# A hybrid encoder block on one core: the input projection by seven block products in place of eight, half of the tokens at a time

## The chip, the core and the metric

The kernel runs on one core of a Trainium2 chip. TensorE (PE in the profile) does matmuls and transposes. VectorE (DVE), ScalarE (ACT) and GpSimd (POOL) do the elementwise work. SyncE (SP) starts most transfers; 16 DMA engines carry them between the device memory (DRAM) and the on-chip buffer SBUF. Matmuls accumulate in PSUM, of which one "bank" here is a tile of 128 partitions by 512 float32.

The metric is device time in microseconds of one execution, lower is better. Before the change the median is 2041.7 us over 3 runs (2040.75 to 2042.08).

## The reference

x is 2048 tokens by 1024 channels, w_in has 7168 columns.

```python
h = rms_norm(x, pre_norm_w)
proj = h @ w_in
hy_in, hy_gate, sg_u, sg_v, sg_gate = split(proj, [3*1024, 4*1024, 5*1024, 6*1024])
x0, x1, v = split(short_conv_centred(hy_in, conv_w, conv_b), 3)   # 3 taps along the tokens
k = hyena_filter(...)              # a sine MLP of the position times a decay, both directions
y_a = x0 * long_conv_bidir(v * x1, k, hyena_skip) * silu(hy_gate)  # by Fourier transform
vn = layer_norm(sg_v per head of 128) * w + b
mixed = einsum(sgu_w, vn) + sgu_b  # 128 x 128 mixing of positions in chunks of 128 tokens
y_b = sg_u * mixed * silu(sg_gate)
y = concatenate([y_a, y_b]) @ w_out
out = x + rms_norm(y, post_norm_w)
```

## The kernel before

**Products.** Every wide product is made at more than single-pass precision: `split` (line 147) makes a rounded high part on ACT (line 150) and the remainder on DVE or POOL (line 152), and `mm3` (lines 155 to 159) runs three matmuls, high by high, low by high, high by low. One matmul is 128 x 128 stationary by 128 x 512 moving.

**Projection.** w_in is cut into 56 blocks of 128 output channels. `prep_w` loads a block (512 KB) and splits it, the remainder on POOL. The normalised, transposed x stays in SBUF in four token quarters, `xh[n]` and `xl[n]`. `project(blk, nxt)` takes a block over the quarters in turn: 8 slices of the 1024 input channels, three matmuls each, 24 into one bank, then the consumer reads the bank. That is 96 matmuls a block and 5376 in all.

**Stages.** `x_phase` normalises 16 tiles of 128 tokens on DVE (line 288), transposes them on PE (line 293) and splits them; two blocks run between (`ug_first`). `mlp` makes the hidden layers of the filter. `ug_phase` projects sg_gate and sg_u with `k1_jobs` beside it: 32 jobs, each two filter products (line 454), decay (line 456), sum and difference, l1 norm (line 463, DVE), first Fourier step, result to the DRAM array AK. `xv_phase` projects x1 and v, convolves (line 501), and a first Fourier step sends the product to AU. `xg_phase` does x0 and hy_gate, result to XG. `vb_phase` projects sg_v, normalises (lines 644 to 652), mixes (line 660), and multiplies by the stored sg_u product (line 619). In its background and behind half of `xv_phase`, from `late_jobs`, are 64 `fft_job`s (second Fourier step of AU and of AK, pointwise product on lines 691 and 695, inverse step, to BY) and 32 `inv_job`s (last step, transposed on line 733, times XG, to Y). `first_out` and `out_phase` multiply Y by w_out (1536 matmuls), normalise and add x.

**What sets the order.** The jobs are generators; at each yield of the projection `run` calls `tick`, which moves every active job on by one step and starts `rate` new ones. From there the order of the instructions on each engine is fixed in the program: each engine takes its own row strictly in order, and waits at a semaphore where an operand isn't there. DMAs that SP starts go in one order too.

## Time and profile before

| of the profiled execution | value |
|---|---|
| its own time | 2044.02 us |
| span, first to last instruction | 2042.2 us |
| median of the runs that were timed | 2041.7 us |
| PE busy | 1991.0 us, 97% |
| DVE busy | 1160.2 us, 57% |
| ACT busy | 764.4 us, 37% |
| POOL busy | 230.0 us, 11% |
| moved by DMA | 274.22 MB, mean 134 GB/s |
| granted TensorE clock, mean | 0.995 |

The profiled execution takes 1.8 us more than its span, and 2.3 us more than the median. "Busy" counts an engine as busy from an instruction's start to its end; matmuls overlap, so a matmul of 0.39 us can start 0.23 us behind the last. In rows of a timeline stand the start, the length, the engine, the line, the operation, output<-inputs by the program's names, the shape and a count, and in brackets how long the engine was idle before and what ended it.

### The profile page before, as it was taken

To read this page: it belongs to the slowest core of one execution; us is meant where nothing else is said; L and a number is where in the kernel's file an instruction comes from. 1 tells how busy PE (TensorE), PEld (TensorE's weight loads), DVE (VectorE), ACT (ScalarE), POOL (GpSimd) and SP (SyncE) were. 2 spreads that over 40 slices of the span, in tenths; PEclk is the share of its full clock that TensorE was granted. 3 is DMA by queue.
4 is the path that set the end of the run, shared out by engine and by line. 5 is a ranking of instruction groups with operands and counts; after the bars stand their busy time and mean duration, and the time that the engine had idled before them with its cause. 6 is when DMAs were issued, how large, how long until landed. Compare 5 with 4: busy or idle time off the path is not lost. (4 is left out here: it accounts for less than half of the span.)

```text
span 2042.2 us, 24620 instructions
## 1 busy us (share of the span) xinstructions
PE 1991.0 (97%) x9000; PEld 1618.6 (79%) x9000; DVE 1160.2 (57%) x1906; ACT 764.4 (37%) x1333; POOL 230.0 (11%) x227
## 2 busy tenths in 40 slices
PE   6999999999999999999999999999999999999998
PEld 5777888878888877777777778788788887888887
DVE  7357555663333587778877766665666664323221
ACT  7134434443333455555444444433222343211111
POOL 1011111111000010111111101110000000101000
PEclk9999999999999999999999999999999999999999
DMA  6155535441222455546554455443546555523311
GB/s 214 49 147 179 164 119 171 157 131 47 61 61 62 127 157 153 154 125 191 154 155 140 144 160 166 152 145 117 160 144 200 159 171 172 171 83 97 110 62 42
DMA packets 189705, 274.22 MB, mean 134 GB/s; under 512 B 18027, under 2 KB 93803, under 8 KB 189551
## 3 DMA queue, kind: packets, MB, share of 16 engines
q1 hardware_dynamic: 175184, 250.56, 38.9%
q0 software_dynamic: 14112, 21.50, 4.3%
q8 instruction: 71, 1.16, 0.2%
q10 hardware_dynamic: 288, 0.59, 0.1%
q14 instruction: 50, 0.41, 0.1%
HBM read 179.26 MB, written 93.33 MB: 133 GB/s over the span
## 5 line engine op out<-in xcount | busy, mean ns | idle before, releaser
L157 PE MATMUL proj<-xh,hi 128*128 128x512 f32 x1792 | 708.8, 396 | 0.0
L158 PE MATMUL proj<-xh,lo 128*128 128x512 f32 x1792 | 704.1, 393 | 0.0
L159 PE MATMUL proj<-xl,hi 128*128 128x512 f32 x1792 | 703.5, 393 | 0.0
L159 PEld LDWEIGHTS proj<-xl,hi 128*128 128x128 f32 x1792 | 337.8, 189 | 70.3 <-issue 0.5
L158 PEld LDWEIGHTS proj<-xh,lo 128*128 128x128 f32 x1792 | 338.3, 189 | 69.2 <-issue 1.5
L157 PEld LDWEIGHTS proj<-xh,hi 128*128 128x128 f32 x1792 | 338.1, 189 | 68.3 <-issue 0.7
L152 POOL TENSOR_TENSOR lo<-wraw,hi 128x1024 fp32r<-128x1024 f32 x56 | 135.7, 2422 | 602.2 <-ACT hi L150 602.0
L158 PE MATMUL proj<-woh,q 128*128 128x512 f32 x448 | 174.4, 389 | 0.0
L159 PE MATMUL proj<-wol,q 128*128 128x512 f32 x448 | 174.3, 389 | 0.0
L157 PE MATMUL proj<-woh,q 128*128 128x512 f32 x448 | 174.1, 389 | 0.0
L152 DVE TENSOR_TENSOR lo<-raw,hi 128x512 fp32r<-128x512 f32 x192 | 133.4, 720 | 45.5 <-ACT hi L150 45.1
L501 DVE SCALAR_TENSOR_TENSOR t<-raw,cw,t 128x512 f32<-128x512 f32 x96 | 80.3, 840 | 109.5 <-ACT raw L492 54.4
L150 ACT CAST hi<-raw 128x512 fp32r<-128x512 f32 x192 | 111.9, 621 | 30.6 <-DMA raw<-BY 24.4
L509 ACT COPY raw<-proj 128x512 f32<-128x512 f32 x96 | 56.1, 585 | 165.3 <-PE proj L159 165.2
L150 ACT CAST hi<-pa 128x512 fp32r<-128x512 f32 x64 | 39.7, 620 | 199.6 <-DVE pa L695 186.9
L150 ACT CAST hi<-wraw 128x1024 fp32r<-128x1024 f32 x55 | 57.9, 1052 | 133.3 <-PE proj L158 83.9
L691 DVE TENSOR_TENSOR pa<-u,b 64x512 f32<-64x512 f32 x128 | 87.6, 684 | 35.3 <-PE b L159 18.6
L157 PEld LDWEIGHTS proj<-woh,q 128*128 128x128 f32 x448 | 84.1, 188 | 17.6
L158 PEld LDWEIGHTS proj<-woh,q 128*128 128x128 f32 x448 | 84.1, 188 | 17.5 <-DVE q L803 0.3
L159 PEld LDWEIGHTS proj<-wol,q 128*128 128x128 f32 x448 | 84.1, 188 | 17.5
L691 DVE TENSOR_TENSOR pb<-u,b 64x512 f32<-64x512 f32 x128 | 87.9, 686 | 1.9
L157 PE MATMUL b<-hi,tv 128*128 128x512 f32 x192 | 80.7, 420 | 7.9 <-ACT hi L150 6.4
(161 smaller groups left out, 2512.9 us busy)
## 6 DMA issues: line engine op xcount, KB each, us to landing
wraw<-in_w_in_dram SPq DMA_DIRECT2D x56, 512.0 KB, 3.8
xt<-in_x_dram SPq DMA_DIRECT2D x32, 512.0 KB, 5.0
dd<-in_c_dec_dram SPq DMA_DIRECT2D x32, 512.0 KB, 4.3
AK<-ev SPq DMA_DIRECT2D x64, 256.0 KB, 3.6
tv<-in_c_tv_dram POOLq DMA_DIRECT2D x64, 256.0 KB, 4.3
AU<-ev SPq DMA_DIRECT2D x64, 256.0 KB, 2.8
raw<-AU SPq DMA_DIRECT2D x64, 256.0 KB, 4.2
raw<-AK SPq DMA_DIRECT2D x64, 256.0 KB, 3.6
```

The costliest lines, as they stand in the source:

```text
L150: (copy or self.nc.scalar.copy)(hi, raw)
L152: eng.tensor_tensor(lo, raw, hi.bitcast(F32), op=ALU.subtract)
L157: t.matmul(ps, sh, mh, start=first, stop=False)
L158: t.matmul(ps, sl, mh, start=False, stop=False)
L159: t.matmul(ps, sh, ml, start=False, stop=last)
L501: nc.vector.scalar_tensor_tensor(v, raw[:, j0:j0 + 4], wv(0), v, op0=ALU.mult, op1=ALU.add)
L509: self.nc.scalar.copy(raw[:, 1 + 4 * n:5 + 4 * n].rearrange("q j p -> q (j p)"), ps)
L691: nc.vector.tensor_tensor(o, uu, kk, op=ALU.mult)
```

## The change

**Seven products.** Blocks are taken in pairs, and the tokens in two halves of 1024 (positions 0 to 63 and 64 to 127 of each of 16 groups). With two blocks of weights, two halves of the input channels and two token groups of 512, a pair is a 2 x 2 by 2 x 2 product of blocks. Winograd's form of Strassen's scheme makes it with seven block products of sums and differences. A block product is 4 slices times three matmuls, 12 matmuls, so a pair takes 84 per token half, and 28 pairs by 2 halves take 4704 matmuls in place of 5376.

- The seven x factors of a half (`x_factors`) are made on DVE from the transposed tiles, split by ACT with the remainders on DVE (three) and POOL (four). They lie as 4 groups of 128 tokens, so a matmul's moving operand is 4 runs of 128 columns, where before it was one run of 512. The second half's factors are made during U(0) (`x_jobs`), stored in XS, and loaded (7 x 2 MB) as the last pair of the first half lets go of each.
- The seven weight factors of a pair: four sums on POOL (`prep_begin`), then seven splits, high part on ACT, remainder on POOL (0, 2, 5) or DVE (1, 3, 4, 6). Factors 1, 3, 4, 6 are written to DRAM (WS, 512 KB each, 112 of them) and read back in the second half; the others are made a second time there.
- `stream` runs products 0, 1, 2, 3, 4 of a pair, and 5 and 6 behind product 0 of the next. Partial sums are copied out of a bank by ACT (`snap`, three a pair) and added by DVE (`add`, three a pair).

**Order of the stages.** B is sg_gate with sg_u, U is x1 with v, G is x0 with hy_gate, V is two heads of sg_v. First half: `x_phase` for its 8 tiles, B(0) with the k1 jobs, U(0) with `x_jobs`, G(0) and V(0). Second half: U(1), G(1), B(1), V(1), then the output projection.

**Filter's second step.** It is a job of its own (`kfft_job`, 64), in the background of G(0), V(0) and U(1), and goes by DRAM (KF, 64 x 256 KB written and read); `fft_job` loads it. The 64 `fft_job`s and 32 `inv_job`s are all in the background of the last stage (G(1), B(1), V(1)).

**Small moves.** The l1 sum of `k1_job` goes from DVE to POOL. `run` ticks at every second yield. PSUM banks: proj 4, a 2, b 2 in place of 3, 2, 3. The output of the x1 by v product of the first half goes by DRAM (U0), and the convolutions keep edge columns between the halves.

```diff
--- before.py
+++ after.py
+UNITS = range(7)
+
+SLOT = (0, 5, 1, 4, 2, 3, 6)
+SPILL = (1, 3, 4, 6)
...
+class TakeG(Take):
+    def c11(self, A, s1):
+        self.r0 = self.b.wide([128, 18, 64], "r0")
+        self.b.add(self.r0[:, 1:9].rearrange("q j p -> q (j p)"), A, s1)
+
+    def c22(self, C, u3):
+        self.sg = self.b.wide([128, 1024], "sg")
+        s = self.sg[:, 512:]
+        self.b.add(s, C, u3)
+        self.nc.scalar.activation(s, s, AF.Silu)
+
+    def c21(self, B):
+        self.nc.scalar.activation(self.sg[:, :512], B, AF.Silu)
+
+    def c12(self, C, u2):
+        self.b.add(self.r0[:, 9:17].rearrange("q j p -> q (j p)"), C, u2)
+        self.b.go(self.b.g_job(self.h, self.c, self.r0, self.sg))
...
     def run(self, fg):
-        for _ in fg:
-            self.tick()
+        for n, _ in enumerate(fg):
+            if n % 2:
+                self.tick()
...
     def bank(self, tag):
-        return self.pp.tile([128, 512], F32, tag=tag, name=tag, bufs={"proj": 3, "a": 2, "b": 3}[tag])
+        return self.pp.tile([128, 512], F32, tag=tag, name=tag, bufs={"proj": 4, "a": 2, "b": 2}[tag])
...
+            self.order = B(0) + U(0) + G(0) + V(0) + U(1) + G(1) + B(1)[:7] + V(1) + B(1)[7:]
...
+                        self.background(self.k1_jobs(kp), 1.3)
+                        self.run(self.stream(8))
...
+                    self.background(self.x_jobs(1), 0.25)
+                    self.run(self.stream(8))
...
+                    self.background(kfft, 1.0)
+                    self.run(self.stream(12, 1))
...
+                    self.background(self.fft_jobs(), 1.35)
+                    self.run(self.stream(20, "wo"))
...
+    def x_factors(self, raw, put, xts):
+        nc = self.nc
+        tt = nc.vector.tensor_tensor
+        b12 = self.x_turn(xts[1], 0, "a")
+        r12 = raw("r12")
+        nc.scalar.copy(r12, b12)
+        b11 = self.x_turn(xts[0], 0, "b")
+        put(0, b11, nc.vector)
+        t1 = raw("t1")
+        tt(t1, r12, b11, op=ALU.subtract)
+        b22 = self.x_turn(xts[1], 1, "a")
+        t2 = raw("t2")
+        tt(t2, b22, t1, op=ALU.subtract)
+        put(1, t2, nc.gpsimd)
+        b21 = self.x_turn(xts[0], 1, "b")
+        put(2, b21, nc.vector)
+        put(3, t1, nc.gpsimd)
+        t3 = raw("t3")
+        tt(t3, b22, r12, op=ALU.subtract)
+        put(4, t3, nc.gpsimd)
+        t4 = raw("t4")
+        tt(t4, b21, t2, op=ALU.subtract)
+        put(5, t4, nc.gpsimd)
+        put(6, b22, nc.vector)
...
-    def prep_w(self, blk, pool=None, tag="w", bufs=5, copy=None):
...
-    def project(self, blk, nxt):
...
+    def prep_begin(self, n):
+        nc = self.nc
+        if n >= len(self.order):
+            return None
+        h, kind, c, b1, b2 = self.order[n]
+        raw = self.rp.tile([128, 7, 512], F32, name="wraw", tag="wraw")
+        w = self.i["w_in"]
+        again = (kind, c) in self.seen
+        self.seen.add((kind, c))
+        nc.sync.dma_start(raw[:, 0:2].rearrange("p q c -> p (q c)"), w[b1].rearrange("p k c -> p (k c)"))
+        if again:
+            nc.sync.dma_start(raw[:, 3], w[b2, :, 4:8].rearrange("p k c -> p (k c)"))
+        else:
+            nc.sync.dma_start(raw[:, 2:4].rearrange("p q c -> p (q c)"), w[b2].rearrange("p k c -> p (k c)"))
+            tt = nc.gpsimd.tensor_tensor
+            tt(raw[:, 4], raw[:, 2], raw[:, 3], op=ALU.add)
+            tt(raw[:, 5], raw[:, 4], raw[:, 0], op=ALU.subtract)
+            tt(raw[:, 2], raw[:, 0], raw[:, 2], op=ALU.subtract)
+            tt(raw[:, 6], raw[:, 1], raw[:, 5], op=ALU.subtract)
+        return (kind, c), raw, again, []
+    def prep_unit(self, rec):
+        if rec is None or len(rec[3]) == 7:
+            return
+        nc = self.nc
+        key, raw, again, units = rec
+        u = len(units)
+        w = self.wp.tile([128, 2, 512], F32R, name="wu", tag="wu", bufs=5)
+        if again and u in SPILL:
+            nc.sync.dma_start(w.bitcast(F32), self.WS[key][SPILL.index(u)])
+        else:
+            src = raw[:, SLOT[u]]
+            nc.scalar.copy(w[:, 0], src)
+            eng = nc.gpsimd if u in (0, 2, 5) else nc.vector
+            eng.tensor_tensor(w[:, 1], src, w[:, 0].bitcast(F32), op=ALU.subtract)
+            if u in SPILL and not again:
+                nc.sync.dma_start(self.WS[key][SPILL.index(u)], w.bitcast(F32))
+        units.append(w)
+    def snap(self, ps, tag):
+        s = self.rp.tile([128, 512], F32, name="sn", tag=tag)
+        self.nc.scalar.copy(s, ps)
+        return s
+    def add(self, out, ps, sn, view=lambda v: v):
+        self.nc.vector.tensor_tensor(out, view(ps), view(sn), op=ALU.add)
+    def product(self, x, w, u, ps, first=True, last=True):
+        po = ps.rearrange("q (i t) -> q i t", i=4)
+        for k in range(4):
+            c = slice(k * 128, k * 128 + 128)
+            self.mm3(po, w[u][:, 0, c], w[u][:, 1, c], x[u][:, 0, :, c], x[u][:, 1, :, c],
+                     first and k == 0, k == 3, skip_group_check=True)
+    def finish_pair(self, new):
+        if self.prev is None:
+            return
+        x, w, take, B, C, u2 = self.prev
+        self.prev = None
+        self.product(x, w, 5, B, first=False)
+        take.c21(B)
+        self.reload(new, 5)
+        yield
+        self.product(x, w, 6, C, first=False)
+        take.c12(C, u2)
+        self.reload(new, 6)
+        yield
+    def reload(self, new, u):
+        if new == "wo":
+            self.load_wo(u)
+        elif new is not None:
+            self.load_x(u)
+    def stream(self, pairs, new=None):
+        for n in range(pairs):
+            h, kind, c, b1, b2 = self.order[self.at]
+            take = {"U": TakeU, "G": TakeG, "B": TakeB, "V": TakeV}[kind](self, h, c)
+            key, _, _, w = self.next_w
+            x, rec = dict(self.X), self.next_w
+            change = new if n == pairs - 1 else None
+            while not w:
+                self.prep_unit(rec)
+            B = self.bank("proj")
+            self.product(x, w, 0, B)
+            s1 = self.snap(B, "s1")
+            self.reload(change, 0)
+            while len(w) < 7:
+                self.prep_unit(rec)
+            self.at += 1
+            self.next_w = self.prep_begin(self.at)
+            yield
+            yield from self.finish_pair(None)
+            self.product(x, w, 1, B, first=False)
+            u2 = self.snap(B, "s2")
+            self.reload(change, 1)
+            self.prep_unit(self.next_w)
+            yield
+            A = self.bank("proj")
+            self.product(x, w, 2, A)
+            take.c11(A, s1)
+            self.reload(change, 2)
+            self.prep_unit(self.next_w)
+            yield
+            C = self.bank("proj")
+            self.product(x, w, 3, C)
+            self.reload(change, 3)
+            self.prep_unit(self.next_w)
+            yield
+            self.product(x, w, 4, B, first=False)
+            u3 = self.snap(B, "s1")
+            take.c22(C, u3)
+            self.reload(change, 4)
+            self.prep_unit(self.next_w)
+            yield
+            self.prev = (x, w, take, B, C, u2)
+            if n == pairs - 1:
+                yield from self.finish_pair(change)
...
-        nc.vector.tensor_tensor(l1, l1, dd, op=ALU.add)
+        nc.gpsimd.tensor_tensor(l1, l1, dd, op=ALU.add)
...
+    def kfft_jobs(self):
+        for hf in range(2):
+            for g in range(32):
+                yield self.kfft_job(g, hf)
+    def fft_raw(self, g, hf, src):
+        raw = self.ld("raw")
+        self.nc.sync.dma_start(raw, src[8 * g:8 * g + 8, :, hf * 512:hf * 512 + 512].rearrange("r j c -> (r j) c"))
+        return raw
+    def kfft_job(self, g, hf):
+        nc = self.nc
+        tv = self.fp.tile([128, 2, 128], F32R, name="tk", bufs=2)
+        nc.gpsimd.dma_start(tv, self.i["c_tv"][g][:, 0:2])
+        raw = self.fft_raw(g, hf, self.AK)
+        yield
+        hi, lo = self.fsplit(nc.vector, raw)
+        yield
+        ps = self.bank("b")
+        self.mm3(ps, tv[:, 0], tv[:, 1], hi, lo)
+        ev = self.f("ev")
+        nc.scalar.copy(ev, ps)
+        nc.sync.dma_start(self.KF[hf, g], ev)
...
     def fft_job(self, g, hf):
         nc = self.nc
-        rows, cs = slice(8 * g, 8 * g + 8), slice(hf * 512, hf * 512 + 512)
         tv = self.fp.tile([128, 4, 128], F32R, name="tv", bufs=2)
         nc.gpsimd.dma_start(tv, self.i["c_tv"][g])
-        raws = []
-        for src in (self.AU, self.AK):
-            raw = self.ld("raw")
-            nc.sync.dma_start(raw, src[rows, :, cs].rearrange("r j c -> (r j) c"))
-            raws.append(raw)
-        yield
-        parts = [self.fsplit(e, raw) for e, raw in zip((nc.vector, nc.vector), raws)]
-        yield
-        spec = []
-        for hi, lo in parts:
-            ps = self.bank("b")
-            self.mm3(ps, tv[:, 0], tv[:, 1], hi, lo)
-            spec.append(ps)
-        u = self.f("u")
-        nc.scalar.copy(u, spec[0])
-        k = spec[1]
+        raw = self.fft_raw(g, hf, self.AU)
+        k = self.ld("k")
+        nc.sync.dma_start(k, self.KF[hf, g])
+        yield
+        hi, lo = self.fsplit(nc.vector, raw)
+        yield
+        u = self.bank("b")
+        self.mm3(u, tv[:, 0], tv[:, 1], hi, lo)
```

Three places in the rows of the engines. On PE, the start of the program: the transposes of x (`xt`, line 293 before, 415 after) and the first products (lines 157 to 159 before, 271 to 273 after; `hi`, `lo` and `wu` are weights). Before:

```order
L293 MATMUL b_244<-ident_72,xt_116 128x128 x4
L293 MATMUL a_237<-ident_72,xt_116 128x128 x4
L157 MATMUL proj_494<-xh0_85,hi_108 128x512
L158 MATMUL proj_494<-xh0_85,lo_110 128x512
L157 MATMUL proj_521<-xh0_85,hi_120 128x512
L158 MATMUL proj_521<-xh0_85,lo_122 128x512
L159 MATMUL proj_494<-xl0_86,hi_108 128x512
```

After:

```order
L415 MATMUL b_338<-ident_75,xt_153 128x128 x4
L415 MATMUL a_329<-ident_75,xt_156 128x128 x4
L415 MATMUL b_380<-ident_75,xt_159 128x128 x4
L271 MATMUL proj_576<-x0_133,wu_573 128x512
L272 MATMUL proj_576<-x0_133,wu_573 128x512
L415 MATMUL a_373<-ident_75,xt_162 128x128 x4
L415 MATMUL a_389<-ident_75,xt_162 128x128 x4
L415 MATMUL b_398<-ident_75,xt_159 128x128 x4
L273 MATMUL proj_576<-x0_133,wu_573 128x512
```

Before, the first product stands behind the transposes of five of sixteen tiles. Now it stands behind those of six tiles and half of the seventh, of the eight of its half, since its moving operand spans all four steps of `x_phase`.

On POOL, the stretch with the k1 jobs (`gd` and `dd` belong to a k1 job, `wraw` and `wu` are weights). Before:

```order
L446 DMA gd_2157<-GD_70 128x256
L152 TENSOR_TENSOR lo_2240<-wraw_2236,hi_2238 128x1024
L446 DMA gd_2381<-GD_70 128x256
L446 DMA gd_2440<-GD_70 128x256
L437 MEMSET lo_2223 64x512
```

After:

```order
L535 TENSOR_TENSOR wu_1433<-wraw_1277,wu_1433 128x512
L735 TENSOR_TENSOR l1_653<-l1_653,dd_1139 128x1024
L516 TENSOR_TENSOR wraw_1277<-wraw_1277 128x512
L517 TENSOR_TENSOR wraw_1277<-wraw_1277 128x512
L518 TENSOR_TENSOR wraw_1277<-wraw_1277 128x512
L519 TENSOR_TENSOR wraw_1277<-wraw_1277 128x512
L718 DMA gd_1415<-GD_72 128x256
L735 TENSOR_TENSOR l1_653<-l1_653,dd_1229 128x1024
L535 TENSOR_TENSOR wu_1523<-wraw_1277,wu_1523 128x512
```

Before, POOL has one remainder a block and the loads of `gd`. Now the l1 sums (line 735), the weight sums (lines 516 to 519) and the weight remainders (line 535) stand between the loads of `gd`.

On DVE, the pointwise products of the Fourier jobs (lines 691 and 695 before, 955 and 959 after; line 152 before and 266 after are remainders). Before:

```order
L695 SCALAR_TENSOR_TENSOR pa_9017<-pb_9018,sgn_195,pa_9017 128x512
L152 TENSOR_TENSOR lo_9026<-pa_9017,hi_9024 128x512
L152 TENSOR_TENSOR lo_9030<-raw_8971,hi_9028 128x512
L152 TENSOR_TENSOR lo_9034<-raw_8973,hi_9032 128x512
L691 TENSOR_TENSOR pa_9085<-u_9083,b_9079 64x512 x2
L691 TENSOR_TENSOR pb_9086<-u_9083,b_9079 64x512 x2
```

After, in the last stage:

```order
L266 TENSOR_TENSOR lo_11315<-raw_11234,hi_11313 128x512
L955 TENSOR_TENSOR pa_11380<-b_11376,k_11236 64x512 x2
L955 TENSOR_TENSOR pb_11381<-b_11376,k_11236 64x512 x2
L547 TENSOR_TENSOR sg_11998<-proj_12003,sn_11929 128x512
L959 SCALAR_TENSOR_TENSOR pa_11380<-pb_11381,sgn_165,pa_11380 128x512
L180 TENSOR_TENSOR ug_12078<-ug_12078,sg_11998 128x512
```

One of two remainders a job is gone from here (it is in `kfft_job`), and the additions of the pairs (line 547, and line 180 of a B pair) stand between the steps of a job.

535 lines of the change are left out of this document (295 added, 240 removed).

## Prediction

> **What bounds the kernel now.** I read the page's busy times first, then windows by stage, then timelines. The page:
>
> ```profile
> span 2042.2 us, 24620 instructions
> PE 1991.0 (97%) x9000; PEld 1618.6 (79%) x9000; DVE 1160.2 (57%) x1906; ACT 764.4 (37%) x1333; POOL 230.0 (11%) x227
> ```
>
> PE is the only engine that is never free. "Busy" overstates it, since matmuls overlap; their pitch says more. A timeline of PE:
>
> ```profile
> 131.08 0.39 PE L159 MATMUL proj<-xl,hi 128*128 128x512 f32 x1
> ...
> 137.20 0.39 PE L159 MATMUL proj<-xl,hi 128*128 128x512 f32 x1
> ```
>
> These stand 27 matmuls apart: 6.12 / 27 = 0.2267 us each, though each lasts 0.39. Four transposes take 0.44 us from the first to the next operation, 0.11 each:
>
> ```profile
> 1423.63 0.60 PE L733 MATMUL a<-ident,y 128*128 128x128 f32 x4
> 1424.07 0.38 PE L640 MATMUL a<-ident,vr 128*128 128x128 f32 x2
> ```
>
> Windows by stage (length; then busy us and count of PE, PEld, DVE, ACT, POOL; clock, DMA share, GB/s), and below them the same two windows with the transposes alone, and with the mixing matmuls (line 657) alone:
>
> ```profile
> 10.00:15.00 5.00, 0.33 (x2) 0.00 (x0) 3.88 (x4) 4.26 (x10) 3.38 (x2) 1.00 1.02 387
> 140.00:420.00 280.00, 275.11 (x1189) 223.71 (x1189) 173.91 (x235) 118.49 (x179) 41.23 (x44) 0.99 0.51 164
> 700.00:1250.00 550.00, 536.20 (x2333) 423.69 (x2333) 421.01 (x590) 268.63 (x485) 71.28 (x95) 1.00 0.51 152
> 1250.00:1690.00 440.00, 432.81 (x2146) 359.70 (x2145) 278.56 (x692) 152.39 (x263) 36.36 (x23) 1.00 0.52 159
> 1690.00:2042.00 352.00, 345.14 (x1519) 284.38 (x1517) 97.62 (x121) 64.80 (x119) 33.51 (x14) 1.00 0.31 103
> ```
>
> ```profile
> 700.00:1250.00 550.00, 11.48 (x76) 1.00 0.51 152
> 1250.00:1690.00 440.00, 34.87 (x240) 1.00 0.52 159
> ```
>
> ```profile
> 1250.00:1690.00 440.00, 42.70 (x256) 1.00 0.52 159
> ```
>
> Count times pitch shows what PE loses. In 700 to 1250: (2333 - 76) x 0.2267 + 76 x 0.11 = 520 of 550, 30 lost (5%), with DVE at 77%. In 1250 to 1690: (2146 - 240 - 256) x 0.2267 + 496 x 0.11 = 429 of 440; the mixing matmuls are few columns but some of their records are a second pass, so I take 11 to 18, say 15. In 140 to 420, the k1 jobs: 1189 x 0.2267 = 270 of 280, 10 lost. In 1690 to 2042, with DVE at 28%, 1519 x 0.2267 = 344 of 352, and that has the tail in it. So PE bounds, and it loses where DVE is near 80%.
>
> **What the change takes away.** 5376 - 4704 = 672 matmuls x 0.2267 = 152.3 us of PE. One small thing is added:
>
> ```profile
> L594 PE MATMUL a<-sw,ones 128*128 128x128 f32 x16 | 3.0, 272 | 0.0
> ```
>
> These 16 records are the eight sums of the mixing weights, each of two passes; they are now made once a half, 3.0 more. All of PE's other work only moves. Net -149.3.
>
> **The front.** Now the first product starts at 25.17, and DVE starts normalising at 7.02:
>
> ```profile
> 7.02 1.28 DVE L288 SCALAR_TENSOR_TENSOR xt<-xt,rs,pw 128x1024 f32<-128x1024 f32 x1 [0.54 <-DMA pw<-in_pre_norm_w_dram]
> 11.85 2.35 POOL L152 TENSOR_TENSOR lo<-wraw,hi 128x1024 fp32r<-128x1024 f32 x1
> 12.40 2.88 DVE L288 SCALAR_TENSOR_TENSOR xt<-xt,rs,pw 128x1024 f32<-128x1024 f32 x1
> 25.17 0.78 PE L157 MATMUL proj<-xh,hi 128*128 128x512 f32 x1
> ```
>
> The new first product needs the first factor of all four steps: DVE has 8 normalisations x 1.28 + 7 operations x 0.61 in each of three steps before it, 23 us, and up to 8 us go where POOL, which now has four remainders a step, holds it up as in the third row (2.88 for 1.28). So it starts near 40: +15 (8 to 25).
>
> **DVE and POOL together.** This is the price that I weigh most. One place:
>
> ```profile
> 916.70 2.41 POOL L152 TENSOR_TENSOR lo<-wraw,hi 128x1024 fp32r<-128x1024 f32 x1 [8.96 <-ACT hi L150]
> ...
> 917.65 2.01 DVE L152 TENSOR_TENSOR lo<-pa,hi 128x512 fp32r<-128x512 f32 x1 [1.16 <-ACT hi L150]
> ```
>
> ```profile
> 906.26 1.28 DVE L152 TENSOR_TENSOR lo<-raw,hi 128x512 fp32r<-128x512 f32 x2
> 907.47 0.68 DVE L551 TENSOR_TENSOR ul<-a,uh 128x512 fp32r<-128x512 f32 x1
> ```
>
> ```profile
> 914.32 1.39 DVE L691 TENSOR_TENSOR pb<-u,b 64x512 f32<-64x512 f32 x2
> 915.74 0.75 DVE L695 SCALAR_TENSOR_TENSOR pa<-pb,sgn,pa 128x512 f32<-128x512 f32 x1
> ```
>
> ```profile
> L152 POOL TENSOR_TENSOR lo<-wraw,hi 128x1024 fp32r<-128x1024 f32 x56 | 135.7, 2422 | 602.2 <-ACT hi L150 602.0
> L691 DVE TENSOR_TENSOR pa<-u,b 64x512 f32<-64x512 f32 x128 | 87.6, 684 | 35.3 <-PE b L159 18.6 <-ACT u L686 14.8
> L695 DVE SCALAR_TENSOR_TENSOR pa<-pb,sgn,pa 128x512 f32<-128x512 f32 x64 | 56.3, 880 | 2.3
> ```
>
> DVE's operation of 917.65, both of whose inputs are in SBUF, began inside POOL's and ended 0.55 after it (919.66 against 919.11): it did its work once POOL was done. Alone such an operation costs 0.605 (906.26 to 907.47 for two). Operations with one input in PSUM show nothing of this: 684 mean over 128 of them, against 880 for line 695, which has two in SBUF and lasts 0.75 alone.
>
> The Trainium skill, "SBUF — State Buffer", Who interferes with whom, says the same as a rule: a VectorE instruction with two SBUF inputs and a GpSimd one that reads SBUF exclude each other, and one with at most one such input isn't touched. It speaks against this change, which gives POOL 4 x 28 + 3 x 56 - 56 + 32 + 32 = 288 more such instructions; if it didn't hold, the next part's sum would be bounded by PE's 187 and the forecast would fall by 50.
>
> *Stretch with the k1 jobs* (order: pairs 3 to 8 with 32 jobs). PE: (6 x 84 + 32 x 10) x 0.2267 = 187 us. A job has POOL's l1 sum, 2.42, and four DVE operations of two SBUF inputs, 2.42: 4.84 x 32 = 155. A pair has seven POOL operations of half the length, 8.5, and five such DVE operations, 3.0: 11.5 x 6 = 69. If these exclude each other they take 224; if DVE's PSUM operations (64 + 24, x 0.605 = 53) never fall beside POOL, 277. If nothing excluded, DVE has 149 and PE bounds. I take 237, nearest to the first since the row of 917.65 is of this kind: +50, less the 10 lost now: +40 (-10 to +80). Behind POOL's l1 sum and the weight sums stand the loads of `gd` in POOL's row, so a job's matmuls wait for these.
>
> *U(0), G(0), V(0), U(1).* PE 28 pairs x 84 + 64 x 3 Fourier + 192 matmuls, 2736 x 0.2267 = 620, with transposes and mixing 650. DVE has 3 additions, convolutions and four splits a pair, as dense as in 700 to 1250 now; the same 5%: +33 (15 to 65).
>
> *Loading the second half's x.* 14.7 MB at the 387 GB/s of the window 10 to 15 are 38 us. The last pair of the first half gives 84 x 0.2267 = 19 us of lead, and some 75 Fourier matmuls that stand there 17 more: +5 (0 to 20).
>
> *Last stage.* PE: 20 x 84 + 64 x 6 + 32 x 6 = 2256 x 0.2267 = 511, with transposes and mixing 537. DVE, by the pitches above: a Fourier job two remainders 1.21, four products 2.84 (914.32 to 915.74 for two), one combination 0.75, 4.8 x 64 = 307; an inverse job 1.8 x 32 = 58; a G pair 1.8 of sums and three operations of 1.28, 5.7 x 8 = 45; a B pair 3.0 x 8 = 24; V and w_out by these rows.
>
> ```profile
> L644 DVE BATCH_NORM_STATS2 bs<-a 128x6 f32<-128x128 f32 x128 | 32.5, 277 | 22.3 <-PE a L640 22.3
> L645 DVE BATCH_NORM_AGGREGATE mv<-bs 128x2 f32<-128x6 f32 x128 | 20.2, 170 | 0.0
> L652 DVE TENSOR_SCALAR vn<-a,mv,rs 128x128 f32<-128x128 f32 x128 | 43.7, 404 | 1.1
> L660 DVE SCALAR_TENSOR_TENSOR vr<-b,nw,bi 128x512 f32<-128x512 f32 x32 | 23.9, 748 | 16.6 <-PE b L657 16.6
> L619 DVE TENSOR_TENSOR ug<-ug,vr 128x512 f32<-128x512 f32 x28 | 20.7, 763 | 18.5 <-DMA ug<-UG 7.5 <-issue 6.2 <-DMA Y<-xg 3.0
> L749 DVE TENSOR_TENSOR wol<-wraw,woh 128x1024 fp32r<-128x1024 f32 x16 | 19.4, 1223 | 5.5 <-ACT woh L748 5.4
> ```
>
> Half of the V rows (141) is 70, its sums 7, w_out 19. That is 530, and with POOL's 60 remainders of 1.2 in the way of about a third of it, some 550. Both engines have 540 to 550 to do; at 77% DVE costs PE 5%, at 100% I take 8 to 9%, 585: +45 (0 to 100).
>
> What is lost now in 700 to 1690 goes with the stages that it belongs to: -(30 + 15) = -45.
>
> *Costed at nothing.* A copy out of a bank by ACT:
>
> ```profile
> L509 ACT COPY raw<-proj 128x512 f32<-128x512 f32 x96 | 56.1, 585 | 165.3 <-PE proj L159 165.2
> ```
>
> The 168 copies of partial sums on ACT: the next product into the bank stands two products (5.4 us) behind, for the copy ahead of product 5 one (2.7 us); a copy takes 0.585. If ACT came 1 us late each time it were 168. ACT's sum: 764 + 168 x 0.585 + about 100 for casts - 60 for evictions that are now DVE additions, 900 us, 46%: no bound. KF by DRAM: its jobs stand stages earlier.
>
> **Sum.** 2042.2 - 149.3 + 15 + 40 + 33 + 5 + 45 - 45 = 1985.9 of span. The profiled execution has 1.8 on top and stands 2.3 above the median: 1985.
>
> **Rivals.**
>
> *PE stays the bound* (0.23). If the other engines keep up as they do now, only the front is paid: 2042 - 149 + 15 = 1908. For it: ACT and POOL are idle now, and DVE's row in 140 to 420 is busy 62% and costs just 10. Against: DVE's sum in the last stage.
>
> *Transfers take over, slower* (0.13). The page:
>
> ```profile
> DMA packets 189705, 274.22 MB, mean 134 GB/s; under 512 B 18027, under 2 KB 93803, under 8 KB 189551
> GB/s 214 49 147 179 164 119 171 157 131 47 61 61 62 127 157 153 154 125 191 154 155 140 144 160 166 152 145 117 160 144 200 159 171 172 171 83 97 110 62 42
> ```
>
> The change adds 117 MB of spilled weights (112 x 0.524, out and in), 29 for x, 34 for KF, 22 for second reads of w_in, 17 for U0 and tables: 493 MB. At 2042 us this is 241 GB/s, above the highest 51-us slice (214). It decides below 241: if 225 is what these transfers sustain in one order on one queue, 493 / 0.225 = 2191. Against: the window 10 to 15 moved 387, and one of share 0.51 moved 164, which makes 320 at full share. The Trainium skill, "DMA: Bandwidth & Descriptors", Specifications, asks for 512 bytes and more a transfer for full rate; XG and part of Y are now written 256 bytes at a time where it was 512, which no row here prices.
>
> *Four runs of 128 columns cost PE* (0.05). No row has such a moving operand. If each run cost as a transpose does, 4 x 0.11 - 0.2267 = 0.21 more, 4704 x 0.21 = 1000 us worse; 0.012 a matmul (57 us) would cancel the gain. I take 0, the row 131.08, as the columns within a run are neighbours.
>
> **Chances.** My forecast 0.55 (its own range 1935 to 2040), the rivals 0.23, 0.13, 0.05, and 0.04 for mixtures near no change. About 0.2%, 4 us, is what a measurement can tell from no change. Faster: 0.53 + 0.23 = 0.76; within 0.2%: 0.04; slower: 0.13 + 0.05 + 0.02 = 0.20. The range takes in the second case's floor and the forecast's upper costs: 1895 to 2065; it leaves out the transfers and the four runs, 0.18.
>
> **What would show it.** PE's count down by some 660. Pitch 0.2267 inside a product. First product near 40. In the k1 stretch POOL and DVE taking turns, PE idle some 50 us. In the last stage DVE over 90%. Wrong, if PE loses less than 40 in these two together (then 1908), if PE waits there for DMA, or if pitch inside a product exceeds 0.24.

## The result: slower by a sixth

The changed kernel takes 2382.74 us in the median of 4 runs (2379.65 to 2387.02), the kernel before 2041.89 (2040.75 to 2043.49). The ratio is 1.167, 95% interval 1.1647 to 1.1693. The forecast was 1985 with a range from 1895 to 2065. The profiled execution took 2379.65 us with a span of 2377.6.

The page of the changed kernel, the rows that answer to those of before:

```profile
span 2377.6 us, 25888 instructions
PE 2014.3 (85%) x8344; PEld 1549.2 (65%) x8344; DVE 1402.1 (59%) x2114; ACT 922.6 (39%) x1724; POOL 650.7 (27%) x602
PEclk9989998989899998659999999999997976999999
GB/s 136 152 221 216 212 252 174 227 217 240 176 259 233 270 237 305 291 207 198 201 205 227 272 253 252 270 239 280 301 248 144 214 226 220 127 132 90 98 89 36
DMA packets 318886, 496.10 MB, mean 209 GB/s; under 512 B 109691, under 2 KB 162939, under 8 KB 317823
```

PE has 656 instructions fewer and is idle 15% of the time. No other engine has taken its place: the busiest, DVE, stands at 59%. Windows by stage (length; then busy us and count of PE, PEld, DVE, ACT, POOL; clock, DMA share, GB/s). Their bounds are the starts of every 84th projection matmul, by which one tells the pairs apart, and the end of the last one: up to the first product, B(0), U(0), G(0) with V(0), the first pair of U(1), the next 24 pairs, the last three, the output projection:

```profile
0.00:41.30 41.30, 13.14 (x53) 9.88 (x53) 26.02 (x39) 25.93 (x53) 20.96 (x21) 1.00 0.72 194
41.30:365.50 324.20, 260.93 (x979) 189.21 (x980) 260.00 (x305) 154.79 (x256) 177.16 (x125) 0.93 0.60 198
365.50:622.10 256.60, 204.40 (x787) 154.96 (x786) 163.18 (x167) 117.08 (x241) 120.04 (x110) 0.89 0.61 207
622.10:933.40 311.30, 288.76 (x1283) 229.61 (x1282) 181.22 (x342) 140.12 (x279) 134.40 (x139) 0.98 0.77 249
933.40:1065.40 132.00, 76.62 (x212) 49.36 (x211) 38.38 (x95) 33.87 (x66) 17.43 (x29) 0.64 0.86 271
1065.40:1740.50 675.10, 639.29 (x2748) 493.31 (x2747) 460.81 (x640) 298.87 (x560) 133.86 (x151) 0.99 0.79 244
1740.50:1964.90 224.40, 157.21 (x683) 119.61 (x682) 154.87 (x380) 71.26 (x126) 13.35 (x15) 0.83 0.69 207
1964.90:2377.60 412.70, 373.93 (x1610) 303.31 (x1608) 117.63 (x151) 80.72 (x146) 33.52 (x14) 0.95 0.35 112
```

Count times pitch, as in the prediction (0.2267 us for each of 7544 matmuls of 512 columns, 0.11 for each of 800 of 128 columns), gives PE 1798 us of work, where the same count gave 1949 before: the change took 151 us away, by the sum 149. But PE now loses 579 us of its time, where it lost 93 (2042 less 1949). By place, and by the prediction's terms with what the stage lost before added where a term was a difference:

| place | lost, measured | lost, as predicted |
|---|---|---|
| up to the first product | 36 | 40 |
| B(0), with the k1 jobs | 104 | 50 |
| U(0), G(0), V(0), U(1) without its first pair | 133 | 33 |
| first pair of U(1) | 90 | 5 |
| G(1), B(1), V(1) | 165 | 45 |
| output projection | 52 | 8 |

Two pairs of the last stage carry 100 of its 165: the third of V(1) takes 121 us with 57 us of work, the last of B(1) 73 with 37. A pair's own products are 19 us.

A product that nothing holds up runs at the old pitch (21 matmuls in 4.76 us, 0.2267 each, a timeline of U(0)):

```profile
488.10 0.39 PE L273 MATMUL proj<-x,wu 128*128 128x512 f32 x1
...
492.86 0.39 PE L273 MATMUL proj<-x,wu 128*128 128x512 f32 x1
```

So the four runs of 128 columns cost nothing.

Now a place in U(0) where PE waits, from the same timeline:

```profile
473.78 1.29 POOL L516 TENSOR_TENSOR wraw<-wraw 128x512 f32<-128x512 f32 x1
475.15 1.29 POOL L517 TENSOR_TENSOR wraw<-wraw 128x512 f32<-128x512 f32 x1
...
476.47 1.66 ACT L533 CAST wu<-wraw 128x512 fp32r<-128x512 f32 x3 [4.73 <-POOL wraw L517]
477.12 2.76 DVE L535 TENSOR_TENSOR wu<-wraw,wu 128x512 fp32r<-128x512 f32 x2 [5.49 <-ACT wu L533]
477.62 1.71 POOL L519 TENSOR_TENSOR wraw<-wraw 128x512 f32<-128x512 f32 x1
...
479.30 3.41 POOL L535 TENSOR_TENSOR wu<-wraw,wu 128x512 fp32r<-128x512 f32 x2
...
481.06 0.80 PE L272 MATMUL proj<-x,wu 128*128 128x512 f32 x1 [2.90 <-POOL wu L535]
...
481.66 0.63 PE L271 MATMUL proj<-x,wu 128*128 128x512 f32 x1
482.08 0.63 PE L272 MATMUL proj<-x,wu 128*128 128x512 f32 x1
```

POOL sums, ACT waits for it 4.73 us, DVE waits for ACT 5.49, POOL's remainder comes behind its sums, PE waits 2.90 for that. Four engines, and three of them idle in turn. DVE's two remainders take 2.76 where two took 1.28 (the row of 906.26), with POOL at work beside them. And behind the wait the matmuls stand 0.42 us apart for some 4 us: the clock has dropped.

### The profile page after: what moved, and what is told of

Same layout as the page of the kernel before. It is cut to its first block, busy times and chain, and to the rows that moved or that the text cites. A ratio compares the mean times of both kernels' runs of the same rounds, so it can differ in the third digit from the quotient of the medians.

```text
span 2377.6 us, 25888 instructions
## 1 busy us (share of the span) xinstructions
PE 2014.3 (85%) x8344; PEld 1549.2 (65%) x8344; DVE 1402.1 (59%) x2114; ACT 922.6 (39%) x1724; POOL 650.7 (27%) x602
## 2 busy tenths in 40 slices
DMA packets 318886, 496.10 MB, mean 209 GB/s; under 512 B 109691, under 2 KB 162939, under 8 KB 317823
## 4 chain that ended last, share of the span: by engine, by line
PE 38%; DMA 17%; issue 12%; DVE 9%; POOL 6%; ACT 4%; SPq 1%; DVEq 0%; ACTq 0%; POOLq 0%
PE proj L272 9%; PE proj L271 9%; PE proj L273 9%; DMA wraw<-in_w_in_dram 6%; PE b L271 3%; PE b L273 2%; POOL wu L535 2%; PE b L272 2%; DVE lo L266 1%; DMA wo_raw<-in_w_out_dram 1%; DMA raw<-BY 1%; ACT hi L264 1%; DMA tk<-in_c_tv_dram 1%; DMA tv<-in_c_tv_dram 1%; POOL wraw L516 1%
## 5 line engine op out<-in xcount | busy, mean ns | idle before, releaser
L271 PE MATMUL proj<-x,wu 128*128 128x512 f32 x1568 | 640.9, 410 | 46.6 <-ACT wu L533 17.4
L272 PE MATMUL proj<-x,wu 128*128 128x512 f32 x1568 | 634.9, 405 | 24.8 <-POOL wu L535 24.7
L273 PE MATMUL proj<-x,wu 128*128 128x512 f32 x1568 | 630.6, 402 | 0.0
L535 POOL TENSOR_TENSOR wu<-wraw,wu 128x512 fp32r<-128x512 f32 x168 | 238.1, 1417 | 636.9 <-ACT wu L533 602.9
L271 PEld LDWEIGHTS proj<-x,wu 128*128 128x128 f32 x1568 | 306.7, 196 | 130.5 <-ACT sn L543 26.0
L272 PEld LDWEIGHTS proj<-x,wu 128*128 128x128 f32 x1568 | 306.3, 195 | 96.8 <-POOL wu L535 33.8
L273 PEld LDWEIGHTS proj<-x,wu 128*128 128x128 f32 x1568 | 305.7, 195 | 64.8 <-issue 0.5
L533 ACT CAST wu<-wraw 128x512 fp32r<-128x512 f32 x280 | 169.9, 620 | 319.8 <-PE proj L273 159.7
L271 PE MATMUL proj<-wo,q 128*128 128x512 f32 x448 | 174.2, 389 | 1.1 <-ACT q L1079 1.1
L272 PE MATMUL proj<-wo,q 128*128 128x512 f32 x448 | 174.4, 389 | 0.5 <-DVE q L1080 0.5
L535 DVE TENSOR_TENSOR wu<-wraw,wu 128x512 fp32r<-128x512 f32 x112 | 115.8, 1043 | 93.4 <-ACT wu L533 91.2
L543 ACT COPY sn<-proj 128x512 f32<-128x512 f32 x168 | 97.7, 581 | 113.3 <-PE proj L273 98.6
L273 PE MATMUL proj<-wo,q 128*128 128x512 f32 x336 | 130.7, 389 | 0.0
L955 DVE TENSOR_TENSOR pa<-b,k 64x512 f32<-64x512 f32 x128 | 87.3, 682 | 42.1 <-PE b L273 38.3
L266 DVE TENSOR_TENSOR lo<-s,hi 128x512 fp32r<-128x512 f32 x64 | 96.3, 1511 | 8.1 <-ACT hi L264 7.8
L271 PEld LDWEIGHTS proj<-wo,q 128*128 128x128 f32 x448 | 84.0, 188 | 19.0 <-ACT q L1079 1.6
L272 PEld LDWEIGHTS proj<-wo,q 128*128 128x128 f32 x448 | 84.1, 188 | 18.5 <-DVE q L1080 1.0
```

Source lines behind the costliest of these rows:

```text
L266: eng.tensor_tensor(lo, raw, hi.bitcast(F32), op=ALU.subtract)
L271: t.matmul(ps, sh, mh, start=first, stop=False, **kw)
L272: t.matmul(ps, sl, mh, start=False, stop=False, **kw)
L273: t.matmul(ps, sh, ml, start=False, stop=last, **kw)
L533: nc.scalar.copy(w[:, 0], src)
L535: eng.tensor_tensor(w[:, 1], src, w[:, 0].bitcast(F32), op=ALU.subtract)
```

## Experiments

Each kernel here was run once, beside a run of the kernel before on the same chip, which took 2039 to 2047. I read no difference under 10 us in them. Pairs and losses are those of the table above. Theory 1, from the rows just shown: PE waits for the *chain* of a pair's weights. Theory 2 is the prediction's: *shared work*, DVE and POOL excluding each other.

### One constant weight, the making of weights kept or left out

```diff
-            self.mm3(po, w[u][:, 0, c], w[u][:, 1, c], x[u]...
+            self.mm3(po, self.wc[:, 0, c], self.wc[:, 1, c], x[u]...
```

> Every product uses one weight factor that was made at the start, so the projection is not the reference's; all loads, sums, splits and spills of weights are still done, and nobody on TensorE waits for them. Theory 1, the chain: TensorE waits in the first half because a pair's weights can be begun only when the one raw tile is free (load, sums on POOL, cast, remainder on POOL, one after the other). Then the first half loses 150 us less: about 2230. Theory 2, shared work: VectorE and GpSimd hold each other up, as the prediction had it; their work is unchanged, so at least 2340.

2416 us. The chain as a thing that PE itself waits for is refuted: PE waits for no weights, and it is no faster. (The ring of weight tiles is four for five here and in the next kernel, to make room. Whether that is behind the 33 us more was not tried.)

```diff
     def prep_begin(self, n):
+        if n:
+            return (kind, c), None, False, []
     def prep_unit(self, rec):
+        if rec[3] or self.at:
+            rec[3].append(None)
+            return
```

> As the kernel with one constant weight factor, and the loads, sums, splits and spills of all other weights are left out. Theory 1, the chain: about the same as that kernel, within 40 us of it. Theory 2, shared work: 150 us and more below it, since the seven POOL operations, the seven casts and 3.1 MB a pair are gone.

2176 us. Making the weights, their loads and spills with it, costs 207 us (240 against the kernel with one constant weight), and that kernel says that this isn't PE's own wait for them. So I set up theory 3, *coupled rows*: the weights' steps wait for each other in the rows of ACT, DVE and POOL, and the copies and additions that free PE's banks, and the jobs' steps, stand behind them there. By place, against the table above, PE loses without weights 57 us for 104 in B(0), 30 for 133 in U(0) to U(1) without its first pair (2 of it in G(0) and V(0)), 77 for 90 in the first pair of U(1), 125 for 165 in the last stage, 53 for 52 in the output projection. The seven pairs of U(0) behind the first, first in the changed kernel, then without weights:

```profile
420.30:622.10 201.80, 161.24 (x653) 124.55 (x652) 128.21 (x127) 95.06 (x203) 96.72 (x91) 0.92 0.63 215
```

```profile
366.60:510.20 143.60, 141.43 (x653) 116.80 (x652) 88.75 (x100) 71.39 (x156) 25.31 (x44) 1.00 0.46 156
```

The same 653 PE instructions take 202 or 144 us. But 2176 is still 134 above the kernel before: a second cause stands beside the weights, in the first pair of U(1), the last stage and behind it.

### Order of POOL's work; the l1 sum back on VectorE

```diff
-            tt(raw[:, 4], raw[:, 2], raw[:, 3], op=ALU.add)   # the four sums, in prep_begin
...
         units.append(w)
+        if u == 0 and not again:
+            tt(raw[:, 4], raw[:, 2], raw[:, 3], op=ALU.add)   # the same four
...
```

> The four sums of a pair's weights stand behind the remainder of its first factor on POOL, which needs none of them; the work is the same. Theory 1, the chain: some 5 us of POOL's sums leave the chain to the next pair's first product, 4 us a pair in 23 pairs of the first half: about 2290. Theory 2, shared work: no change, 2370 to 2385.

2397 us. Taking 5 us out of the chain brings nothing, which agrees with the constant weight.

```diff
-        nc.gpsimd.tensor_tensor(l1, l1, dd, op=ALU.add)
+        nc.vector.tensor_tensor(l1, l1, dd, op=ALU.add)
```

> The l1 sum of the k1 jobs is back on VectorE. By the prediction's sum for that stretch, 32 x 2.42 us leave the side where the two engines exclude each other and 32 x 1.22 come in: 38 us less, 2340. If VectorE, busy 83% there, is by itself what the stretch waits for: 20 to 40 us more, 2410.

2372 us, hardly a difference: B(0) takes 304 in place of 324, but U(0) 270 for 257. My price of 38 for this move was too high by far; that DVE alone would be what the stretch waits for is refuted. The remainders of the k1 jobs do get shorter, from 1511 ns to 896, so it was mostly POOL's l1 sum that made them long; but little of the stretch hangs on them.

### The engines' work alone

The kernel without weight making, with as much work on tiles of their own, for which nobody waits.

```diff
+            eng.tensor_tensor(t[:, 0], t[:, 0], t[:, 1], op=ALU.add)   # t: a tile of POOL's own
```

> The kernel without weight making, and on POOL, in the places of the four sums and three remainders of each pair, as many additions of the same size on a tile of their own, for which nobody waits and which wait for nobody. The projection is not the reference's. Theory 2, shared work: the 7 x 28 operations in the first half and 3 x 28 in the second keep VectorE's two-input operations waiting as now, so most of the 207 us come back: over 2300. Theory 3, coupled rows: what costs is that the weights' steps wait for each other and that the partial sums stand behind them in the rows of ACT, VectorE and POOL; then less than 30 us come back: 2180 to 2205.

> The same with the seven casts of a pair on ACT and the four remainders on VectorE as well, each engine on a tile of its own, with no wait between engines; loads and spills are still left out. The projection is not the reference's. Theory 2, shared work: the engines' full work is back, so about 2370. Theory 3, coupled rows: the work alone costs little where no row waits for another: 2190 to 2240.

2425 and 2474 us, and neither tells anything: since nothing tied these operations to a pair, the scheduler put all of them into B(0), which takes 512 and 533 us there, while G(0) loses nothing. A filler has to be tied to its place:

```diff
+        mk = self.rp.tile([128, 1], F32, name="mk", tag="mk", bufs=8)
+        self.nc.scalar.copy(mk, s[:, 0:1])     # a mark, behind each copied partial sum
+        eng.tensor_copy(t[:, 0, 0:1], mk)      # the filler starts from it
```

> The kernel without weight making; POOL does 7 additions of the weights' size a pair in the first half and 3 in the second, each group started by a mark that ACT makes after a partial sum is copied, so that they keep to their pairs. Nobody waits for them. The projection is not the reference's. Theory 2, the two engines exclude each other: VectorE's two-input operations get longer by what they meet, 80 to 140 us in sum, and the time goes from 2176 to 2240 or more. Theory 3, coupled rows: 2176 to 2205.

> The same with 7 copies a pair on ACT and 4 additions on VectorE. Loads, spills and the waits between the engines for weights are still left out, and the projection is not the reference's. Theory 2: 2300 and more, as the engines have all of their work again. Theory 3: under 2250, the rest of the 207 us being the waits of the chain from engine to engine.

2244 with POOL's work, 2266 with all three engines'. So some 68 of the 207 us are POOL's work beside the rest, and 22 more ACT's and DVE's own. (Rather less than more: the marks themselves are 168 small operations on ACT, 32 us, and 168 on POOL, 61 us.) Neither theory alone: shared work is 90, and 117 come only when the steps also wait for each other, with their loads and spills. The same DVE operation (the product in U(0)) without weights and with POOL's filler:

```profile
L809 DVE TENSOR_TENSOR t<-t,t 128x1024 f32<-128x1024 f32 x8 | 9.7, 1216 | 0.2
```

```profile
L823 DVE TENSOR_TENSOR t<-t,t 128x1024 f32<-128x1024 f32 x8 | 14.5, 1813 | 0.2
```

Both inputs are in SBUF, and it takes 1.81 us for 1.22.

### All weight work on VectorE

```diff
-            tt = nc.gpsimd.tensor_tensor
+            tt = nc.vector.tensor_tensor
...
-            eng = nc.gpsimd if u in (0, 2, 5) else nc.vector
+            eng = nc.vector
```

> All sums and remainders of weights on VectorE, none on POOL. The places where the two engines exclude each other go, VectorE gets 112 + 168 operations more, each 0.61 in place of POOL's 1.2: 170 us. Theory 2, shared work: first half better by 40 to 80, 2310. Theory 3, coupled rows: one engine fewer in the chain, but the partial sums stand behind more in VectorE's row: within 30 of the changed kernel.

2314 us, 68 less, as theory 2 had it. All 280 remainders, first of this kernel, then those of the changed one on POOL and on DVE:

```profile
L535 DVE TENSOR_TENSOR wu<-wraw,wu 128x512 fp32r<-128x512 f32 x280 | 193.1, 699 | 103.9 <-ACT wu L533 102.9
```

```profile
L535 POOL TENSOR_TENSOR wu<-wraw,wu 128x512 fp32r<-128x512 f32 x168 | 238.1, 1417 | 636.9 <-ACT wu L533 602.9 <-DMA wraw<-in_w_in_dram 10.2 <-DMA raw<-BY 8.1
L535 DVE TENSOR_TENSOR wu<-wraw,wu 128x512 fp32r<-128x512 f32 x112 | 115.8, 1043 | 93.4 <-ACT wu L533 91.2 <-DMA dd<-in_c_dec_dram 1.8
```

Put on the busier engine, the work costs 193 us where the two engines spent 354 on it, and PE loses less. Not all of the 354 is the two holding each other up: at the prediction's prices for either alone (0.605 on DVE, half of 2.42 on POOL) the split would take 271, by estimate, since POOL is slower at it; 83 are left for that. Spreading the work over two engines was the dearer way.

### A looser chain

```diff
-        raw = self.rp.tile([128, 7, 512], F32, name="wraw", tag="wraw")
+        ra, rb, rt = [self.rp.tile([128, k, 512], ...) for k, s in ((2, "a"), (2, "b"), (3, "t"))]
```

> The one raw tile of a pair becomes three (first block, second block, sums), and the sums stand behind the first factor's remainder on POOL; the work is the same. Of the 207 us that weights cost, 90 came back with the engines' work alone; the rest is then either the chain from engine to engine or the loads and spills. If it is the chain, the next pair's first block can be loaded and its first factor made some 10 us earlier: 40 to 90 less, 2300 to 2340. If it is loads and spills, whose amount is unchanged, within 20 of the changed kernel.

2361 us, 22 less, between what I had set for the two. The single raw tile is a small part. What makes up the other 95 of the 117 (the order of the rows, or 3.1 MB of loads and spills a pair) stays open. The trace of the changed kernel has both in one row: from 41.3 to 933.4 us ACT's casts of weights wait 81.5 us for POOL's sums and 52.6 for the load of a block, which lands 6.1 us after its issue in the median, where it took 3.8 in the kernel before.

```profile
ACT wu L533 <- POOL wraw L517: 81.5, 26, 4.9
ACT wu L533 <- DMA wraw<-in_w_in_dram: 52.6, 19, 6.4
```

### The piled-up Fourier jobs

The second cause. In PE's row 25 jobs of the filter's second step stand in the first pair of U(1); in the third pair of V(1) and the last of B(1) stand other piles, that of V(1) with much of V's own normalising and mixing: PE waits 15 us there for casts of the jobs (`hi`), 19 for V's steps on DVE (`vn`, `bi`). Where the products of the new stage can't start yet, the scheduler fills in jobs.

```diff
-                    self.background(kfft, 1.0)      # G(0), V(0)
+                    self.background(kfft, 1.7)
```

> The filter's second step starts 1.7 jobs a tick in G(0) and V(0) in place of 1.0, so that all 64 stand before the second half's first pair in TensorE's row. If the 25 jobs that stand in that place now cost the 80 us there by their own chain of loads, the pair at the change of halves falls from 132 us to about 60 and the whole by 50 to 70. If the loading of x is what costs, the pair stays above 110 and the whole falls by less than 25.

2381 us. The pair falls from 132 to 61, but G(0) and V(0) take 379 in place of 311: the same jobs cost the same there, though not by the same wait. There PE waits 29.7 us for `tk`, the table of a job, where it waited 3.4 before, by a view of each kernel's G(0) and V(0):

```profile
PE b L271 <- DMA tk<-in_c_tv_dram: 29.7, 18, 5.6
```

```profile
PE b L271 <- DMA tk<-in_c_tv_dram: 3.4, 1, 3.4
```

`tk` has a ring of two tiles in every kernel here, and a longer one was not tried. So moving the jobs is no gain with two.

```diff
-                    self.run(self.stream(12, 1))
+                    self.run(self.stream(12))       # no loading of x
```

> The second half's x factors are not loaded and the first half's are used again, so the output is not the reference's; all else is the same, the 25 jobs of the filter's second step in the first pair of U(1) too. If loading x is what costs there, the pair falls from 132 us to under 70. If the jobs cost, in a row with the store of each ahead of the next load, it stays above 95.

2354 us, the pair 105: loading x is 27, the jobs (with the mixing of V(0) that stands there) the rest.

```diff
-            ... + G(1) + B(1)[:7] + V(1) + B(1)[7:]
+            ... + G(1) + b[:2] + v[:1] + b[2:4] + v[1:2] + b[4:6] + v[2:3] + b[6:7] + v[3:] + b[7:]
```

> The pairs of V in the second half stand apart, between pairs of B, in place of four in a row near the end. If the 121 us of one V pair come from the wide tiles that four V pairs in a row hold, it falls to 30 and the whole by 40 to 60: 2330. If they come from the chain of the Fourier jobs that stand there, these move to another place and the whole stays within 15.

2377 us. The pile of 121 us goes, and comes back as pairs of 62, 48 and 111.

```diff
-        nc.sync.dma_start(self.KF[hf, g], ev)
+        nc.scalar.dma_start(self.KF[hf, g], ev)     # and the stores to AK, AU, BY
```

> The four kinds of stores that follow a copy on ACT (AK, AU, KF, BY) are issued by ACT right behind the copy, in place of SP, where each waited for ACT ahead of the next loads. If the piled-up Fourier jobs (first pair of U(1), one pair of V(1), the last of B(1)) cost 190 us because their loads stand behind those stores on SP, these three fall by half: 80 to 110 less, 2280. If they cost it by their own chain (load, cast, remainder, matmul, copy), less than 30.

2406 us, the pair 135: not the stores' place in SP's order.

```diff
-                    self.nw_, self.nf, self.nl = 4, 8, 2     # stage of U(1)
+                    self.nw_, self.nf, self.nl = 4, 8, 6
```

> In the stage of U(1) the ring of load tiles has 6 in place of 2; nothing else differs, TensorE's row has the same 25 jobs in the first pair. Each such job takes 3 us now; a load lands 3.9 us after its issue and a tile is free after cast and remainder, 1.3 more, so two tiles give a job each 2.6 us. If the ring bounds the jobs, the pair falls from 132 to 100 or less and the whole by 30 to 50: 2340. If the clock, the steps of a job one after the other, or the DMA queue bound them, less than 10.

2384 us, the pair 134: not the load tiles of `raw`. In the last stage they count somewhat:

```diff
+                    self.nw_, self.nf, self.nl = 4, 8, 6     # stage of U(1)
+                    self.nw_, self.nf, self.nl = 4, 10, 9    # last stage
```

> The kernel without weight making (2176), with the room that this leaves given to the load tiles: 6 for 2 in the stage of U(1), 9 for 4 in the last. The projection is not the reference's. If too few load tiles make the piles of Fourier jobs slow, the three places (119, 107 and 71 us) fall to about 90, 75 and 50: 2100. If not, 2165 to 2180.

2137 us, 40 less: the last pair of B(1) 58 for 71, the output projection 397 for 415, but the first pair of U(1) 121 for 119. With 9 load tiles and no weights at all it is still 97 above the kernel before on its chip (2039).

With all these refuted, the rows of the pile itself (timeline of the changed kernel):

```profile
1026.51 0.58 ACT L921 COPY ev<-b 128x512 f32<-128x512 f32 x1 [1.74 <-PE b L273]
...
1026.99 0.62 ACT L264 CAST hi<-raw 128x512 fp32r<-128x512 f32 x1
...
1027.66 0.79 PE L271 MATMUL b<-hi,tk 128*128 128x512 f32 x1 [1.19 <-ACT hi L264]
1028.26 0.63 PE L272 MATMUL b<-hi,tk 128*128 128x512 f32 x1
1028.68 0.63 PE L273 MATMUL b<-lo,tk 128*128 128x512 f32 x1
1029.35 0.58 ACT L921 COPY ev<-b 128x512 f32<-128x512 f32 x1 [1.74 <-PE b L273]
...
1029.83 0.62 ACT L264 CAST hi<-raw 128x512 fp32r<-128x512 f32 x1
...
1031.90 0.77 PE L271 MATMUL b<-hi,tk 128*128 128x512 f32 x1 [2.59 <-DMA tk<-in_c_tv_dram]
```

PE's three matmuls, then ACT's copy of their result, and only behind that copy in ACT's row the cast of the next job, without which PE can't go on: 1026.51 to 1029.35 is 2.84 us a job. The next job's cast shows no wait of its own, so its data were there; ACT's row held it. PE stands at half clock here (0.42 from one matmul to the next). 24 of the 25 jobs stand so, one behind the other; the first of them starts at 979.79, the last at 1057.56. Of the 23 steps between them 11 take 2.81 to 2.86 us, and the mean is 3.38: 79 us in all, for 16 us of PE work at full clock. The median is 2.84 to 2.88 in the kernels without weights, without loading of x, with more load tiles and with stores on ACT too. Four of the steps end with the load of `tk`, as in the last row; that is 9 us of PE's waits here, 26 are for the cast. All of this is read from the rows; a kernel with the casts ahead of the copies wasn't tried. Nor were the fewer PSUM banks of the jobs (b, 2 for 3) and the halved tick, which came with the change, taken back in any run; in this pair no wait of PE ends with a bank coming free.

### The parts together

> Three raw tiles, all weight sums and remainders on VectorE, and the four stores on ACT. If the parts add up: 68 for VectorE, what the two others give by themselves; above 2150 in any case by the sum, so still slower than before (2042), since the drains, the front and the k1 jobs stay.

2303 us (raw tiles, VectorE, stores on ACT).

> Three raw tiles, all weight sums and remainders on VectorE, 6 load tiles in the stage of U(1); the output is the reference's. If the parts add up, 68 for VectorE, 22 for the raw tiles, 30 to 50 for the load tiles: 2240 to 2265. Slower than before in any case.

2304 us (raw tiles, VectorE, load tiles). Both lie 11 below VectorE alone, hardly a difference: the parts don't add up, and no version here beats the kernel before.

## Why the prediction was wrong

Sign and size were wrong. What failed is how the stages were added up, each as the work of its busiest engine and a few per cent: behind B(0) and ahead of the output projection 33 + 5 + 45 us were to be lost, and 133 + 90 + 165 were. Point by point:

- **PE's work**: right. 656 instructions fewer, 1798 us of work, pitch 0.2267.
- **The front**: right in the number, by luck in part. First product at 41.26, "near 40" was said. But DVE starts to normalise at 14.45, where it was 7.02 and the sum kept that: it waits for ACT until 11.04 and then makes three remainders of weights. The 7 us took the place of the 8 that I had set for POOL holding DVE up, of which the rows show little (eight normalisations of 1493 ns in the mean for 1.28 us).

```profile
14.45 1.27 DVE L409 SCALAR_TENSOR_TENSOR xt<-xt,rs,pw 128x1024 f32<-128x1024 f32 x1
...
41.26 0.79 PE L271 MATMUL proj<-x,wu 128*128 128x512 f32 x1 [0.68 <-ACT x L460]
```

- **DVE and POOL**: the mechanism is there, by the 1.81 us for 1.22 above and by the 68 us that POOL's filler costs. The Trainium skill's rule ("SBUF — State Buffer", Who interferes with whom) is borne out by these rows. I priced it mainly for the k1 stretch, which was to lose 50 and lost 104, 57 of it without any weights. The remainders of the k1 jobs did get longer, 1511 ns a piece for 722 before:

```profile
L266 DVE TENSOR_TENSOR lo<-s,hi 128x512 fp32r<-128x512 f32 x64 | 96.3, 1511 | 8.1 <-ACT hi L264 7.8
```

  But of the 207 us that the weights cost, over half isn't this.
- **U(0), G(0), V(0), U(1)** is the step that failed: "as dense as in 700 to 1250 now; the same 5%", 33 us, and 133 were lost. Without weights these stages lose 30, so the 5% held for all the rest, and 103 came with the weights. I compared busy shares. DVE is busy 64% in U(0) and PE loses a third of it. The sum of each engine's work says how long a stage must be at least; how long it is depends on how often a row of one engine waits for another. A pair's weights put 7 casts, 11 elementwise operations and 6 transfers into rows that also carry what PE waits for, and I had costed only their durations. In the kernel before, a block needed one load, one cast and one remainder.
- **Loading x** failed: I took 75 Fourier matmuls as 17 us of cover. They took 79, since each job waited for the one before; the loading itself is 27 of the 90 lost. The work that was to hide the transfer was itself the longest thing there.
- **The last stage** failed the same way: 585 forecast, 709 measured (1256 to 1965). DVE's sum was right (530, measured 531) and not the point: that is 75% of the stage, where I had set over 90% as the sign, and 69% of the last three pairs. Without weights the stage takes 669. Jobs piled up at two places, and at the end there is nothing left to run beside them: the first matmul with w_out stands 54 us behind the last of a pair (2019.22), which adds 44 to the output projection.
- **Costed at nothing**, the copies of partial sums: PE waits 16.6 us for them. The longest groups of its waits over the whole span, and this one (us in total, times, the longest):

```profile
PE b L271 <- ACT hi L264: 102.4, 42, 17.2
PE b L273 <- DVE lo L266: 40.8, 45, 5.0
PE proj L272 <- POOL wu L535: 24.7, 22, 3.5
...
PE proj L271 <- ACT sn L543: 16.6, 17, 1.9
```

  The longest waits are for the steps of the background jobs (`hi`, `lo`), which I had taken for filling.
- **Rivals.** "Transfers take over" had the right sign by a wrong mechanism: the 496 MB are what was worked out (493), but 250 to 300 GB/s went through for long stretches, above the 241 that I set as the break-even, and in U(0) DMA is busy 61%. The packets under 512 bytes are six times as many (109691 for 18027), and still a busy DMA moves as much: 244 GB/s at a share of 0.79 in the windows above, 152 at 0.51 before. What the traces don't exclude is that single loads which land later are a part of the 95 us that stay open. PE as the bound (1908) never came near, even without any weights (2176). The four runs of 128 cost nothing.

None of the rivals was the one that happened: no engine is the bound, and PE waits for steps in the in-order rows of the others. How far it is by work on two engines that hold each other up (68 to 90 us) the runs show; that the rest is rows waiting for each other is read from the waits, and in a run of its own only 22 us of it came back (the looser chain).

## What to carry to other kernels

An edit that saves work on the busiest engine by more steps on the others isn't paid by their busy shares: count how many times each row must wait for another per piece of work, and what stands behind each wait. Work that is to cover a transfer or a drain covers it only if its own chain runs at full speed when it is alone; time one job by its longest cycle through the rows, not by its matmuls. And work that is split over two engines which hold each other up can cost more than on one of them: 280 remainders took 193 us on DVE alone and 354 on DVE and POOL.

## What the runs showed of the hardware

The clock falls with waiting, and so a wait is paid twice. Up to 475.72, ahead of the wait shown above, the matmuls stand 0.23 us apart; then PE has a single one in 5 us, and from 481.06 on they stand 0.42 us apart (481.66 to 482.08), at twice the old pitch, until some 4 us later. In the pile the granted clock is near half for most of its length:

```profile
1020.00:1030.00 10.00, 4.91 (x9) 2.40 (x9) 1.38 (x2) 2.86 (x6) 1.45 (x3) 0.55 0.78 221
1030.00:1040.00 10.00, 4.91 (x9) 2.41 (x9) 2.08 (x3) 3.42 (x7) 1.70 (x4) 0.50 0.81 255
```

Over the span it is 0.929 for 0.995. The Trainium skill, "TensorE: Matmul & The Clock Gate", Part 1, has this rule, with 3.4 us of idling before the drop and as much work before the rise; the rows come near the rise (some 4 us). I had left it out of the sum, as the kernel before hardly shows it behind its front.
